# Large products as two weight tiles taking turns, each as three matmuls of 256 columns

## The chip, the cores and the metric

The kernel runs on one core of one Trainium2 chip. The metric is the device time of one execution in microseconds; three runs of the kernel before gave 2638.32, 2636.36 and 2638.91 (median 2638.32). Five engines work side by side, each with its own queue of instructions: TensorE (PE in the profile, with its weight loads apart as PEld), VectorE (DVE), ScalarE (ACT), GpSimd (POOL) and SyncE (SP), which here only issues DMAs. They wait for each other through semaphores.

## The reference

Two residual layers over 256 tokens of width 2048, in float32, each followed by a gated feed-forward block with a causal convolution. Layer 0 has an RG-LRU group beside an RWKV-7 group, layer 1 an mLSTM.

```python
def rglru_rwkv7_layer(x, norm, w_in, ..., w_out):
    h = rms_norm(x, norm)
    xa, ga, pb = jnp.split(h @ w_in, [A_WIDTH, 2 * A_WIDTH], axis=-1)
    ya = rg_lru(causal_dwconv(xa, ...), ...) * jax.nn.gelu(ga)
    yb = rwkv7_time_mix(pb, ...)
    return x + jnp.concatenate([ya, yb], axis=-1) @ w_out

def mlstm_layer(x, norm, w_in, ..., w_out):
    xm, z = jnp.split(rms_norm(x, norm) @ w_in, [C_WIDTH], axis=-1)
    ...
    return x + (hs * jax.nn.silu(z)) @ w_out

def conv_ffn(x, norm, w_gate, w_up, conv_w, conv_b, w_down):
    h = rms_norm(x, norm)
    u = jax.nn.silu(causal_dwconv(h @ w_gate, conv_w, conv_b)) * (h @ w_up)
    return x + u @ w_down
```

The products with `w_in`, `w_out`, `w_gate`, `w_up` and `w_down` are the large ones: 436 MB of weights, each used once.

## The kernel before

Activations lie transposed, features on the 128 partitions and the T = 256 tokens along the free dimension, in tiles of 128 features. A product of `nk` input tiles by `nm` output tiles takes `nk` x `nm` weight tiles of 128x128. To keep float32 accuracy with float32r operands, weights and activations are split into a rounded part and a rest: `w = hi + lo`, and an activation tile is `x[:, 1]` (rounded) and `x[:, 0]` (rest). Each weight tile adds three products of 256 columns to its output: `hi`·`x0`, `hi`·`x1` and `lo`·`x1`.

`chunk` (L192) loads 16 weight tiles (1 MB) with one DMA of SP into a `raw` buffer (two of them) and splits them in four pieces: ACT copies 512 columns to `wh`, DVE subtracts to `wl` (L201, L202). `wh` and `wl` have two buffers each.

There are three ways to run a product:

- **Wide, one accumulator** (`project` and `flat` with `mm3`, L205): one matmul of 512 columns (`hi` with both halves of x) into a whole `[128, 2, 256]` accumulator, and one of 256 (`lo` with `x1`) into its second half. The two halves are added when the result is drained. Used for the mLSTM's input (`oin`, 64 output tiles of 16) and for the output products (`oout`, 16 of 32; `eoa` and `eob`, 16 of 8 each). The accumulators come from a pool of three (`mm`).
- **Narrow, one accumulator** (`EWIDE` False): three matmuls of 256 columns into one `[128, 256]` sum (L216 to L218). Used for layer 0's input (`ein`, 40 output tiles of 16) and for the low-rank products at the start (`elow`).
- **Wide pairs** (`flat_pairs` with `mm3_pair`, L258): two output tiles at once, with two accumulators: both 512s (L263), then both 256s (L265). Used for the feed-forward block: `fgu` (gate and up, 44 pairs of 16) and `fd` (down, 8 pairs of 44), in both layers. Their accumulators are a pool of two pairs (`mp`).

Draining a wide result into an activation (`scaled`, L365) takes an ACT copy of one half, a DVE addition of the other and a DVE multiplication by `rstd`; a narrow one takes the multiplication alone. `add_residual` (L382) takes two DVE additions for a wide result and one for a narrow one.

The recurrences run as generators: after every fourth weight tile `tick` lets each of them emit its next piece, so that their small products stand between the large ones on TensorE. `finish` ticks with no large products in between; `even` calls it for the last RWKV pairs between `eoa` and `eob`. A scheduler then sets each engine's order; it moves instructions past each other where their operands allow.

At the start (`load_x`, L128) the four pieces of x and the four `elow` chunks are loaded in turns by SP. GpSimd squares x and sums the squares for the norm.

Of the kernel before, what the change touches and what calls it, by code (L numbers as in the profile page):

```python
# [24 lines left out]
P = 128  # L25
# [19 lines left out]
EWIDE = False  # L45
# [3 lines left out]
AWAITS = [0, 4, 0, 1, 1, 3]  # L49

# [56 lines left out]
class Builder:  # L107
# [115 lines left out]
    def project(self, src, wide=True):  # L223

        w = self.chunk(src)
        ps = self.psum_mm()
        ps = ps if wide else ps[:, 0]
        for k in range(KD):
            self.mm3(ps, w, slice(k * P, k * P + P), self.x[k], k == 0, k == KD - 1)
            if k % TICK == TICK - 1:  # L230
                self.tick()
        return ps

    def projections(self, src, n, wide=True):

        ahead = [self.project(src[i], wide) for i in range(2)]
        yield from ahead
        for i in range(2, n):
            yield self.project(src[i], wide)

    def flat(self, src, nk, nm, x, done):

        w, ps = None, None
        for i in range(nm * nk):
            m, k = divmod(i, nk)
            if i % 16 == 0:
                w = self.chunk(src[i // 16])
            if k == 0:
                ps = self.psum_mm()
            c = i % 16 * P  # L250
            self.mm3(ps, w, slice(c, c + P), x[k], k == 0, k == nk - 1)
            if k == nk - 1:
                done(m, ps)
            if i % TICK == TICK - 1:
                self.tick()


    def mm3_pair(self, ps, w, c, x, start, stop):  # L258
        TE = self.nc.tensor
        hi = [w[0][:, i:i + P] for i in c]  # L260
        lo = [w[1][:, i:i + P] for i in c]
        for i in range(2):
            TE.matmul(ps[:, i], hi[i], x, start=start, stop=False)  # L263
        for i in range(2):
            TE.matmul(ps[:, i, 1], lo[i], x[:, 1], start=False, stop=stop)  # L265

    def flat_pairs(self, src, nk, npair, x, pool):

        w, ps = None, None
        for i in range(npair * nk):  # L270
            k = i % nk
            if i % 8 == 0:
                w = self.chunk(src[i // 8])
            if k == 0:
                ps = pool.tile([P, 2, 2, T], F32, name=self.name("mp"), tag="mp")
            c = i % 8 * 2 * P
            self.mm3_pair(ps, w, (c, c + P), x[k], k == 0, k == nk - 1)
            if i % 2 == 1:
                self.tick()
            if k == nk - 1:  # L280
                yield ps
# [100 lines left out]
    def add_residual(self, m, ps, gain):  # L382
        for i in range(2):
            self.nc.vector.tensor_tensor(out=self.res[m], in0=ps[:, i], in1=self.res[m], op=ALU.add)  # L384
        if gain is not False:
            self.norm_tile(m, gain)


    def ffn(self, l, gain):
        nc, tc = self.nc, self.tc  # L390
        with ExitStack() as es:
            big = es.enter_context(self.tile_pool(name=f"ffn{l}", bufs=1))
            tmp = es.enter_context(self.tile_pool(name=f"ffnt{l}", bufs=2))
            nps = es.enter_context(self.tile_pool(name=f"ffn_ps{l}", bufs=1, space=PSUM))
            pps = es.enter_context(self.tile_pool(name=f"ffn_pp{l}", bufs=2, space=PSUM))
# [4 lines left out]
            ahead = [next(pairs) for _ in range(2)]  # L400
            for f, ps in enumerate(chain(ahead, pairs)):
                g = self.scaled(tmp, ps[:, 0], 2, "g")
                c = self.conv(tmp, g, 3, f"f_conv_w{l}", NF, f"f_conv_b{l}", f, "cv")
                nc.scalar.activation(c, c, AF.Silu)
                u = self.scaled(tmp, ps[:, 1], 0, "u")
                nc.vector.tensor_tensor(out=u, in0=u, in1=c, op=ALU.mult)
                ux.append(big.tile([P, 2, T], F32R, name=self.name("ux"), tag=f"u{f}"))
                self.split(u, ux[f])
            for m, ps in enumerate(self.flat_pairs(self.io[f"fd{l}"], NF, KD // 2, ux, pps)):
                for i in range(2):  # L410
                    self.add_residual(2 * m + i, ps[:, i], gain)


    def even(self, gain):
        nc, tc = self.nc, self.tc
        with ExitStack() as es:
# [14 lines left out]
            ps = self.projections(ein, 40, EWIDE)  # L431
# [368 lines left out]
    def odd(self, gain, folded, fold_pool):  # L800
# [3 lines left out]
        with ExitStack() as es:  # L804
# [5 lines left out]
            with ExitStack() as e1:  # L810
# [9 lines left out]
                ps = self.projections(io["oin"], CHEADS * CTILES)  # L820
# [14 lines left out]
            with ExitStack() as e2:  # L835
# [7 lines left out]
                nums = self.start(self.heads_out(one, sml, pw, pst, gates, raws, vs, xcs, zs, big_tile, yx))  # L843
                for ct in range(CHEADS * CTILES):
                    while len(zs) >= 6:
                        self.tick()
                    z = self.scaled(sml, self.project(io["oin"][32 + ct]), 0, "z", 6)
                    A.activation(z, z, AF.Silu)
                    zs[ct] = z
# [234 lines left out]
def _by_cols(w):  # L1084

    k, m = w.shape
    return np.ascontiguousarray(w.reshape(k // P, P, m // P, P).transpose(2, 1, 0, 3)).reshape(m // P, P, -1)


def _flat(w):  # L1090

    k, m = w.shape
    t = w.reshape(k // P, P, m // P, P).transpose(2, 0, 1, 3).reshape(-1, 16, P, P)
    return np.ascontiguousarray(t.transpose(0, 2, 1, 3)).reshape(-1, P, 2048)


def _pairs(ws):

    n, k, _, _ = ws.shape
    t = ws.reshape(n, k // P, P, 2, P).transpose(0, 1, 3, 2, 4).reshape(-1, 16, P, P)  # L1100
# [9 lines left out]
def _arrange(I):  # L1110
# [16 lines left out]
    o["ein"] = _by_cols(np.concatenate(pieces, 1))  # L1127
    o["eoa"], o["eob"] = _flat(I["even_w_out"][0][:AW]), _flat(I["even_w_out"][0][AW:])
    o["oin"], o["oout"] = _by_cols(I["odd_w_in"][0]), _flat(I["odd_w_out"][0])
    for l in range(2):  # L1130
        by = lambda n: I[n][l].reshape(D, NF, P).transpose(1, 0, 2)
        o[f"fgu{l}"] = _pairs(np.stack([by("ffn_w_gate"), by("ffn_w_up")], 2))
        o[f"fd{l}"] = _pairs(I["ffn_w_down"][l].reshape(DFF, KD // 2, 2, P).transpose(1, 0, 2, 3))
# [43 lines left out]
```

## Time and profile before

| | us |
|---|---|
| median of three runs | 2638.32 |
| profiled execution | 2638.66 |
| its span, first to last instruction | 2636.9 |
| ein and the recurrences of layer 0 | 35 to 388 |
| eoa, eob | 394 to 517 |
| FFN up and down, layer 0 | 517 to 1251 |
| mLSTM: oin, then oout | 1251 to 1885 |
| FFN up and down, layer 1 | 1885 to 2620 |

The page gives each engine's busy time, the span in 40 slices, the chain of work that ended last, and the costliest groups. A row of a group reads: line, engine, operation, out<-in, shapes, count | busy us, mean ns of one | idle time of the engine before it, and what ended that. In the order of time, a row gives start and length in us, then the same names; `x2` says that two equal instructions follow each other. A matmul's record is longer than the distance to the next one, since matmuls are pipelined: distances are read from starts.

### The profile page before, as it was taken

The page shows a single profiled execution, that of the slowest core. Times are in us where ns is not written, and L with a number is a line of the kernel's source. Part 1 is how long each engine was busy: PE and PEld are TensorE (multiplying, and loading weights), DVE is VectorE, ACT ScalarE, POOL GpSimd, SP SyncE. Part 2 cuts the span into 40 slices and gives each one's busy share as a digit, 9 for nine tenths or more (in the row PEclk, how much of TensorE's full clock was granted, in tenths as well). Part 3 has the DMA queues.
Part 4 walks back from the last instruction along what each step waited for, and adds up shares of the span by engine and source line. Part 5 has one row for each costly group of instructions (what it writes and reads, how often), then busy time and mean ns, then how long its engine had stood idle before and what let it go on. Part 6 is the DMA issues. An engine that isn't in the chain of part 4 may idle for free.

```text
span 2636.9 us, 42747 instructions
## 1 busy us (share of the span) xinstructions
PE 2595.7 (98%) x16200; PEld 2274.7 (86%) x16200; DVE 1872.8 (71%) x4251; ACT 1457.9 (55%) x3078; POOL 163.7 (6%) x442
## 2 busy tenths in 40 slices
PE   7999999999999999999999999999999999999997
PEld 7988887888888888888888888888888888888886
DVE  7988888888666666555777788865666677765554
ACT  5766664555555554444666766644455555554443
POOL 4122121000000000000000000000000000000000
PEclk9999999999999999999999999999999999999998
DMA  5433333465555555555444344455555555555553
GB/s 189 155 123 118 128 103 132 169 213 206 188 191 192 192 192 192 192 192 195 147 149 146 136 160 149 155 183 186 191 192 188 186 187 190 187 188 201 180 201 131
DMA packets 67119, 454.38 MB, mean 172 GB/s; under 512 B 9264, under 2 KB 9776, under 8 KB 13664
## 3 DMA queue, kind: packets, MB, share of 16 engines
q1 hardware_dynamic: 62352, 443.78, 47.2%
q0 software_dynamic: 4416, 7.85, 1.1%
q8 instruction: 127, 2.08, 0.3%
q14 instruction: 80, 0.66, 0.1%
q10 hardware_dynamic: 144, 0.01, 0.0%
HBM read 448.70 MB, written 2.10 MB: 171 GB/s over the span
## 4 chain that ended last, share of the span: by engine, by line
PE 81%; DVE 0%; ACT 0%; POOL 0%; issue 0%; DVEq 0%; POOLq 0%
PE mp L263 37%; PE mp L265 19%; PE mm L214 14%; PE mm L212 7%; PE sc L887 1%; PE mm L211 1%; PE pv L872 1%; PE pz L1027 1%; PE pr L881 1%; PE pz L1028 0%; DVE res L1072 0%; PE pz L1005 0%; PE pt L349 0%; PE pt L1041 0%; PE pt L1018 0%; DVE res L384 0%
## 5 line engine op out<-in xcount | busy, mean ns | idle before, releaser
L202 DVE TENSOR_TENSOR wl<-raw,wh 128x512 fp32r<-128x512 f32 (+1 forms) x1680 | 1102.4, 688 | 506.6 <-ACT wh L201 505.5
L201 ACT CAST wh<-raw 128x512 fp32r<-128x512 f32 (+1 forms) x1680 | 954.0, 617 | 729.7 <-PE mp L263 506.6
L263 PE MATMUL mp<-x,wh 128*128 128x512 f32 x2816 | 884.7, 395 | 0.0
L265 PEld LDWEIGHTS mp<-x,wl 128*128 128x128 f32 x2816 | 529.0, 188 | 125.0
L265 PE MATMUL mp<-x,wl 128*128 128x256 f32 x2816 | 553.2, 278 | 0.0
L263 PE MATMUL mp<-ux,wh 128*128 128x512 f32 x1408 | 436.8, 392 | 0.0
L263 PEld LDWEIGHTS mp<-x,wh 128*128 128x128 f32 x2816 | 428.8, 189 | 0.1
L214 PE MATMUL mm<-x,wh 128*128 128x512 f32 x960 | 341.7, 394 | 0.0
L265 PEld LDWEIGHTS mp<-ux,wl 128*128 128x128 f32 x1408 | 264.4, 188 | 58.1
L212 PE MATMUL mm<-x,wl 128*128 128x256 f32 x1024 | 283.4, 287 | 0.0
L265 PE MATMUL mp<-ux,wl 128*128 128x256 f32 x1408 | 277.8, 279 | 0.0
L214 PE MATMUL mm<-yx,wh 128*128 128x512 f32 x720 | 258.2, 398 | 0.0
L212 PE MATMUL mm<-yx,wl 128*128 128x256 f32 x768 | 211.6, 286 | 1.9 <-DVE wl L202 1.0
L263 PEld LDWEIGHTS mp<-ux,wh 128*128 128x128 f32 x1408 | 213.2, 188 | 0.0
L214 PEld LDWEIGHTS mm<-x,wh 128*128 128x128 f32 x960 | 180.2, 188 | 35.9 <-DVE x L296 0.2
L212 PEld LDWEIGHTS mm<-x,wl 128*128 128x128 f32 x1024 | 193.2, 189 | 7.5 <-DVE yx L175 2.3
L216 PE MATMUL mm<-x,wh 128*128 128x256 f32 x640 | 194.5, 304 | 0.0
L218 PE MATMUL mm<-x,wl 128*128 128x256 f32 x640 | 182.9, 286 | 2.3 <-DVE wl L202 2.3
L217 PE MATMUL mm<-x,wh 128*128 128x256 f32 x640 | 181.6, 284 | 0.0
L214 PEld LDWEIGHTS mm<-yx,wh 128*128 128x128 f32 x720 | 136.4, 190 | 29.2 <-DVE yx L175 0.2
L212 PEld LDWEIGHTS mm<-yx,wl 128*128 128x128 f32 x768 | 145.0, 189 | 7.9 <-DVE wl L202 1.6
L216 PEld LDWEIGHTS mm<-x,wh 128*128 128x128 f32 x640 | 122.4, 191 | 6.9
(352 smaller groups left out, 2656.1 us busy)
## 6 DMA issues: line engine op xcount, KB each, us to landing
raw<-fgu SPq DMA_DIRECT2D x176, 1024.0 KB, 4.8
raw<-fd SPq DMA_DIRECT2D x88, 1024.0 KB, 4.8
raw<-oin SPq DMA_DIRECT2D x64, 1024.0 KB, 4.8
raw<-ein SPq DMA_DIRECT2D x40, 1024.0 KB, 4.9
raw<-oout SPq DMA_DIRECT2D x32, 1024.0 KB, 4.8
raw<-eoa SPq DMA_DIRECT2D x8, 1024.0 KB, 4.8
raw<-eob SPq DMA_DIRECT2D x8, 1024.0 KB, 4.8
wif<-wif POOLq DMA_DIRECT2D x12, 256.0 KB, 4.4
```

The lines of the kernel that those rows point to most:

```text
L201: nc.scalar.copy(hi[:, s], raw[:, s])
L202: nc.vector.tensor_tensor(out=lo[:, s], in0=raw[:, s], in1=hi[:, s].bitcast(F32), op=ALU.subtract)
L211: TE.matmul(ps, hi, x, start=True, stop=False)
L212: TE.matmul(ps[:, 1], lo, x[:, 1], start=False, stop=False)
L214: TE.matmul(ps, hi, x, start=False, stop=stop)
L216: TE.matmul(ps, hi, x[:, 0], start=start, stop=False)
L217: TE.matmul(ps, hi, x[:, 1], start=False, stop=False)
L218: TE.matmul(ps, lo, x[:, 1], start=False, stop=stop)
L263: TE.matmul(ps[:, i], hi[i], x, start=start, stop=False)
L265: TE.matmul(ps[:, i, 1], lo[i], x[:, 1], start=False, stop=stop)
L872: TE.matmul(ps[:, s], xm[:, 3 + s * P:3 + s * P + P], bv, start=True, stop=True)
L881: TE.matmul(ps, bl, xc, start=True, stop=True)
```

## The change

All large products but the start's low-rank ones go through one function, `stream`. It walks through `turns`: the second half of one output tile's weight tiles alternates with the first half of the next output tile's. Within a pair of weight tiles the matmuls alternate too. With `WIDE` False each weight tile is three matmuls of 256 columns into one sum. Weights are laid out in memory in that order (`_stream`), and `oin` becomes two streams, `oxm` and `oz`. The feed-forward block uses the common pool of three accumulators instead of pairs. At the start SP loads the first piece of x and ACT's queue the other three, all ahead of the first weight chunk's use, and the squares are ACT's, with the sums on DVE.

```diff
+def turns(n, nk):
+    h = nk // 2
+    for s in range(n + 1):
+        a = [(s - 1, k) for k in range(h, nk)] if s else []
+        b = [(s, k) for k in range(h)] if s < n else []
+        yield from zip(a, b) if a and b else ((t,) for t in a + b)
...
         for i in range(4):
-            nc.sync.dma_start(out=res[:, 4 * i:4 * i + 4], in_=self.io["xT"][:, 4 * i:4 * i + 4])
+            (nc.scalar if i else nc.sync).dma_start(out=res[:, 4 * i:4 * i + 4], in_=self.io["xT"][:, 4 * i:4 * i + 4])
+        for i in range(4):
             hi, lo = self.chunk(low[i], 4 * w, 4)
             for k in range(4 * i, 4 * i + 4):
                 self.operand(k, gain)
-                self.square(k, nc.gpsimd)
+                self.square(k)
...
+    def stream(self, src, n, nk, x):
+        TE = self.nc.tensor
+        ps, w, at = {}, None, 0
+        for step in turns(n, nk):
+            ops = []
+            for m, k in step:
+                if at % 16 == 0:
+                    w = self.chunk(src[at // 16])
+                c = slice(at % 16 * P, at % 16 * P + P)
+                at += 1
+                if k == 0:
+                    ps[m] = self.psum_mm()
+                ops.append(self.parts_of(ps[m], (w[0][:, c], w[1][:, c]), x[k], k == 0, k == nk - 1))
+            for group in zip(*ops):
+                for out, lhsT, rhs, start, stop in group:
+                    TE.matmul(out, lhsT, rhs, start=start, stop=stop)
+            if at % TICK == 0:
+                self.tick()
+            for m, k in step:
+                if k == nk - 1:
+                    yield ps.pop(m)
+
+    def parts_of(self, ps, w, x, first, last):
+        hi, lo = w
+        if WIDE:
+            return [(ps, hi, x, first, False), (ps[:, 1], lo, x[:, 1], False, last)]
+        ps = ps[:, 0]
+        return [(ps, hi, x[:, 0], first, False), (ps, hi, x[:, 1], False, False), (ps, lo, x[:, 1], False, last)]
...
     def add_residual(self, m, ps, gain):
-        for i in range(2):
-            self.nc.vector.tensor_tensor(out=self.res[m], in0=ps[:, i], in1=self.res[m], op=ALU.add)
+        for p in [ps[:, i] for i in range(2)] if WIDE else [ps]:
+            self.nc.vector.tensor_tensor(out=self.res[m], in0=p, in1=self.res[m], op=ALU.add)
...
-            pairs = self.flat_pairs(self.io[f"fgu{l}"], KD, NF, self.x, pps)
+            ps = self.projections(self.io[f"fgu{l}"], 2 * NF)
...
-            for m, ps in enumerate(self.flat_pairs(self.io[f"fd{l}"], NF, KD // 2, ux, pps)):
-                for i in range(2):
-                    self.add_residual(2 * m + i, ps[:, i], gain)
+            self.flat(self.io[f"fd{l}"], NF, KD, ux, lambda m, ps: self.add_residual(m, ps, gain))
```

How that moves instructions is seen on three engines. On TensorE, in layer 0's FFN up, before (an `mp` is an accumulator pair, `x2` are its two halves, a `wh` and its `wl` hold one chunk):

```order
L263 MATMUL mp_6921<-x_6713,wh_6956 128x512 x2
L265 MATMUL mp_6921<-x_6713,wl_6957 128x256 x2
L263 MATMUL mp_6921<-x_6750,wh_6956 128x512 x2
L265 MATMUL mp_6921<-x_6750,wl_6957 128x256 x2
L263 MATMUL mp_6921<-x_6775,wh_6956 128x512 x2
L265 MATMUL mp_6921<-x_6775,wl_6957 128x256 x2
```

And now, in the same product (an `mm` is one output tile's sum):

```order
L249 MATMUL mm_7130<-x_6449,wh_7089 128x256
L249 MATMUL mm_7062<-x_6752,wh_7089 128x256
L249 MATMUL mm_7130<-x_6449,wh_7089 128x256
L249 MATMUL mm_7062<-x_6752,wl_7090 128x256
L249 MATMUL mm_7130<-x_6449,wl_7090 128x256
L249 MATMUL mm_7062<-x_6796,wh_7089 128x256
L249 MATMUL mm_7130<-x_6492,wh_7089 128x256
```

Four matmuls for two weight tiles have become six, and the two sums that alternate are half an output tile apart in k.

On SP, at the start of the program, before (`xT` is x, `elow` the low-rank weights, `vec` and `con_even` vectors and constants):

```order
L138 DMA res<-xT 128x1024
L195 DMA raw_100<-elow 128x1152
L138 DMA res<-xT 128x1024
L195 DMA raw_172<-elow 128x1152
L138 DMA res<-xT 128x1024
L195 DMA raw_245<-elow 128x1152
L138 DMA res<-xT 128x1024
L195 DMA raw_318<-elow 128x1152
```

And now:

```order
L147 DMA res<-xT 128x1024
L205 DMA raw_103<-elow 128x1152
L205 DMA raw_174<-elow 128x1152
L164 DMA vec_sb<-vec 128x787
L176 DMA con_even_sb<-con_even 128x900
L449 DMA lora_612<-lora 128x256
L205 DMA raw_246<-elow 128x1152
L205 DMA raw_318<-elow 128x1152
```

Three loads of x are gone from SP (they are ACT's second to fourth instructions), and three others stand ahead of the third weight chunk.

On DVE, at the end of eoa, before (L384 adds eoa's results to `res`, `s`, `x` and `uv` belong to a round of the last RWKV pair, L202 splits weights of eob):

```order
L674 TENSOR_TENSOR x_1042_6185<-pc_6186,mv_5544 128x64
L202 TENSOR_TENSOR wl_6289<-raw_6286,wh_6288 128x512
L384 TENSOR_TENSOR res<-mm_6176,res 128x256
L679 COPY uv_5387<-pc_6200 64x64
L384 TENSOR_TENSOR res<-mm_6176,res 128x256
L680 COPY uv_5387<-pc_6200 64x64
L202 TENSOR_TENSOR wl_6350<-raw_6347,wh_6349 128x512
L696 SCALAR_TENSOR_TENSOR s_1046_6208<-pc_6205,pc_5204,sd_6210 64x64 x2
```

And now, around eoa's last result:

```order
L666 TENSOR_TENSOR x_1035_6257<-pc_6258,mv_5577 128x64
L381 TENSOR_TENSOR res<-mm_6187,res 128x256
L671 COPY uv_5467<-pc_6274 64x64
L672 COPY uv_5467<-pc_6274 64x64
L381 TENSOR_TENSOR res<-mm_6244,res 128x256
L688 SCALAR_TENSOR_TENSOR s_1039_6295<-pc_6292,pc_5229,sd_6297 64x64 x2
L212 TENSOR_TENSOR wl_6470<-raw_6467,wh_6469 128x512
L666 TENSOR_TENSOR x_1042_6307<-pc_6308,mv_5577 128x64
```

The round's `x_1042` stood ahead of eoa's last result and now stands behind it.

More of the change, by code (lines that the diff above doesn't have):

```diff
@@ L44 @@
 ZSTEP = 7
-EWIDE = False
+WIDE = False
 PIECES = 4
@@ new lines, in parts_of, with result, projections @@
+    def parts_of(self, ps, w, x, first, last):
[4 more added lines that the diff above has]
+        return [(ps, hi, x[:, 0], first, False), (ps, hi, x[:, 1], False, False), (ps, lo, x[:, 1], False, last)]
+    def result(self, ps):
+        return ps if WIDE else ps[:, 0]
+    def projections(self, src, n):
+        g = self.stream(src, n, KD, self.x)
+        ahead = [self.result(next(g)) for i in range(2)]
@@ L237, in projections @@
         yield from ahead
-        for i in range(2, n):
-            yield self.project(src[i], wide)
+        for ps in g:
+            yield self.result(ps)
     def flat(self, src, nk, nm, x, done):
[L243 to L255, printed above, removed]
@@ L258, in mm3_pair @@
[L258 to L261, printed above, removed]
-        for i in range(2):
-            TE.matmul(ps[:, i], hi[i], x, start=start, stop=False)
-        for i in range(2):
[L265 to L281, printed above, removed]
+        for m, ps in enumerate(self.stream(src, nm, nk, x)):
+            done(m, self.result(ps))
@@ L430, in even @@
             self.load_con("con_even", E, nc.sync)
-            ps = self.projections(ein, 40, EWIDE)
+            ps = self.projections(ein, 40)
             ahead = next(ps)
@@ L846, in odd @@
                         self.tick()
-                    z = self.scaled(sml, self.project(io["oin"][32 + ct]), 0, "z", 6)
+                    z = self.scaled(sml, self.result(next(ps)), 0, "z", 6)
                     A.activation(z, z, AF.Silu)
@@ L1080, in trunk_kernel, with _stream @@
     Builder(tc, io, ctx).build()
-def _by_cols(w):
+def _stream(w):
     k, m = w.shape
[L1087 to L1100, printed above, removed]
+    t = w.reshape(k // P, P, m // P, P).transpose(2, 0, 1, 3)
+    i = np.array([x for step in turns(m // P, k // P) for x in step])
+    t = t[i[:, 0], i[:, 1]].reshape(-1, 16, P, P)
     return np.ascontiguousarray(t.transpose(0, 2, 1, 3)).reshape(-1, P, 2048)
@@ L1126, in _arrange @@
         pieces += [w[:, cols(j)], w[:, AW + j * P:AW + j * P + P]]
-    o["ein"] = _by_cols(np.concatenate(pieces, 1))
-    o["eoa"], o["eob"] = _flat(I["even_w_out"][0][:AW]), _flat(I["even_w_out"][0][AW:])
-    o["oin"], o["oout"] = _by_cols(I["odd_w_in"][0]), _flat(I["odd_w_out"][0])
+    o["ein"] = _stream(np.concatenate(pieces, 1))
+    o["eoa"], o["eob"] = _stream(I["even_w_out"][0][:AW]), _stream(I["even_w_out"][0][AW:])
+    o["oxm"], o["oz"] = _stream(I["odd_w_in"][0][:, :CW]), _stream(I["odd_w_in"][0][:, CW:])
+    o["oout"] = _stream(I["odd_w_out"][0])
     for l in range(2):
-        by = lambda n: I[n][l].reshape(D, NF, P).transpose(1, 0, 2)
-        o[f"fgu{l}"] = _pairs(np.stack([by("ffn_w_gate"), by("ffn_w_up")], 2))
-        o[f"fd{l}"] = _pairs(I["ffn_w_down"][l].reshape(DFF, KD // 2, 2, P).transpose(1, 0, 2, 3))
+        gu = np.stack([I[n][l].reshape(D, NF, P) for n in ("ffn_w_gate", "ffn_w_up")], 2)
+        o[f"fgu{l}"], o[f"fd{l}"] = _stream(gu.reshape(D, 2 * DFF)), _stream(I["ffn_w_down"][l])
     lora = z(8, P, 4, P)
```

25 lines of the change are left out of this document (6 added, 19 removed).

## The prediction

> **What bounds the kernel now.** I read the page from its busy times to its chain, then the busy time by stage, then single matmuls in order of time.
>
> ```profile
> span 2636.9 us, 42747 instructions
> PE 2595.7 (98%) x16200; PEld 2274.7 (86%) x16200; DVE 1872.8 (71%) x4251; ACT 1457.9 (55%) x3078; POOL 163.7 (6%) x442
> PE   7999999999999999999999999999999999999997
> PEld 7988887888888888888888888888888888888886
> PEclk9999999999999999999999999999999999999998
> PE 81%; DVE 0%; ACT 0%; POOL 0%; issue 0%; DVEq 0%; POOLq 0%
> ```
>
> TensorE is busy in every slice but the first and the last, at the full granted clock, and the chain that ended last runs through almost nothing else. So time is matmuls times their spacing; what other engines save is hidden. Each matmul has a weight load of its own (16200 of both). The busy time is no measure of spacing, as records overlap, so I count records in stretches of one kind of work:
>
> ```profile
> core 0: us, PE busy (x) PEld busy (x) DVE busy (x) ACT busy (x) POOL busy (x), PEclk, DMA share, GB/s
> 83.00:95.00 12.00, 12.00 (x103) 12.00 (x102) 10.58 (x32) 7.41 (x14) 1.83 (x5) 1.00 0.45 129
> 520.00:1000.00 480.00, 480.00 (x2761) 418.95 (x2760) 355.69 (x753) 267.71 (x562) 11.40 (x55) 1.00 0.56 198
> 1010.00:1250.00 240.00, 240.00 (x1393) 211.34 (x1392) 131.97 (x237) 106.97 (x206) 0.77 (x3) 1.00 0.54 191
> 1720.00:1880.00 160.00, 160.00 (x914) 139.80 (x913) 92.99 (x172) 71.53 (x142) 0.00 (x0) 1.00 0.55 192
> ```
>
> The rows are: ein (already three matmuls of 256 columns per weight tile), FFN up, FFN down (both pairs of wide tiles), and oout (wide tiles, one accumulator). A record is counted if it touches the stretch, so the count belongs to the stretch plus one record (0.28 us in ein, 0.34 on average elsewhere). That gives 12.28/103 = 0.119 us a matmul in ein, 480.34/2761 = 0.1740 in FFN up, 240.34/1393 = 0.1725 in FFN down, 160.34/914 = 0.1754 in oout. Per 128x128 weight tile, with three matmuls in ein and two elsewhere: **ein 0.358, FFN up 0.348, FFN down 0.345, oout 0.351 us.** In ein, weight loading alone fills the whole stretch; elsewhere it leaves an eighth free.
>
> **The change part by part.** The products hold 6,656 weight tiles: FFN up 2,816, FFN down 1,408, oin 1,024, ein 640, oout 512, eoa and eob 256. All but ein go from a 512-column and a 256-column matmul to three of 256. The columns stay at 768 a tile; what is added is 6,016 matmuls, each with a weight load. So one number decides: the spacing of 256-column matmuls that alternate between two accumulators and follow each other without a wider one between. Nothing in this trace is exactly that. The nearest rows:
>
> ```profile
> 60.20 0.28 PE L217 MATMUL mm<-x,wh 128*128 128x256 f32 x1
> 60.31 0.27 PE L218 MATMUL mm<-x,wl 128*128 128x256 f32 x1
> 60.43 0.28 PE L216 MATMUL mm<-x,wh 128*128 128x256 f32 x1
> ...
> 62.10 0.28 PE L218 MATMUL mm<-x,wl 128*128 128x256 f32 x1
> 62.22 0.28 PE L216 MATMUL mm<-x,wh 128*128 128x256 f32 x1
> 62.34 0.28 PE L217 MATMUL mm<-x,wh 128*128 128x256 f32 x1
> ```
>
> ein, one accumulator: just after a break 0.115, but after some seven matmuls it settles at 0.120 and stays.
>
> ```profile
> 18.40 0.28 PE L216 MATMUL pc<-x,wh 128*128 128x256 f32 x1
> ...
> 20.88 0.28 PE L216 MATMUL pc<-x,wh 128*128 128x256 f32 x1
> ```
>
> The low-rank products at the start, three accumulators by turns of three: 21 matmuls in 2.48 us, 0.118; but a third of their loads bring 32 columns only.
>
> ```profile
> 1000.20 0.40 PE L265 MATMUL mp<-x,wl 128*128 128x256 f32 x2
> 1000.43 0.63 PE L263 MATMUL mp<-x,wh 128*128 128x512 f32 x2
> 1000.90 0.39 PE L265 MATMUL mp<-x,wl 128*128 128x256 f32 x2
> 1001.13 0.62 PE L263 MATMUL mp<-x,wh 128*128 128x512 f32 x2
> ```
>
> FFN up: two of 256 on alternating accumulators take 0.23, 0.116 each; but two of 512 went ahead of them, 0.235 each, twice the time their loads need.
>
> ```profile
> L263 PEld LDWEIGHTS mp<-x,wh 128*128 128x128 f32 x2816 | 428.8, 189 | 0.1
> ...
> 301.92 0.96 PEld L602 LDWEIGHTS pw<-ar,bk 64*128 64x128 f32 x8
> ```
>
> Small 128-column products: eight loads, the last starting (0.96-0.19)/7 = 0.110 after the one before (one load's record lasts 189 ns). The bounds are thus 0.110 and 0.120. **I take 0.120**, 0.360 a tile: of these rows ein alone has nothing but full loads and 256 columns for longer than ten matmuls, and the faster ones come behind a break or wide matmuls, when loads have had time to spare. Two accumulators then change nothing, as the load is what is full.
>
> Terms: FFN up 2,816 x (0.360-0.348) = +34 us; FFN down 1,408 x (0.360-0.345) = +21; oin, oout, eoa, eob 1,792 x (0.360-0.351) = +16 (oin and eo are mixed with small products, so I use oout's figure). Ein 0. Sum +71.
>
> The Trainium skill, in "TensorE: Matmul & The Clock Gate", section "Back-to-back issue gap", spaces matmuls by N/2.4 + 2.5 ns, 216 for 512 columns and 109 for 256; by it a tile would go from 325 to 328 ns, and the sum would be +15 us instead of +71. The 0.235 and 0.120 above are both longer than it says. Its page "Perfetto Trace Analysis", section "Optimizing Tensor Performance", holds that "Larger matmuls are more efficient than smaller matmuls, when possible", which speaks against the change; the FFN rows show no such gain (0.235 against twice 0.116), the ein rows a small one (twice 0.120).
>
> **The start.** Now x arrives in four pieces behind weight chunks, and ein runs freely from 37.90.
>
> ```profile
> 11.65 0.33 SPq L195 DMA_DIRECT2D raw<-elow  x1
> 37.90 0.39 PE L218 MATMUL mm<-x,wl 128*128 128x256 f32 x1 [2.28 <-DVE wl L202]
> L202 DVE TENSOR_TENSOR wl<-raw,wh 128x512 fp32r<-128x512 f32 x1664 | 1089.6, 686 | 506.6 <-ACT wh L201 505.5
> L296 DVE SCALAR_TENSOR_TENSOR x<-res,vec_sb,x 128x256 fp32r<-128x256 f32 x64 | 36.1, 578 | 7.8 <-ACT x L295 7.5
> L311 DVE TENSOR_TENSOR ssq<-ssq,sq 128x256 f32<-128x256 f32 x60 | 25.1, 419 | 1.4 <-ACT sq L309 1.4
> L202 DVE TENSOR_TENSOR wl<-raw,wh 128x288 fp32r<-128x288 f32 x16 | 12.8, 856 | 0.0
> 7.32 0.89 DVE L296 SCALAR_TENSOR_TENSOR x<-res,vec_sb,x 128x256 fp32r<-128x256 f32 x1 [7.32 <-ACT x L295]
> ```
>
> Afterwards the squares leave GpSimd for ACT and their sums go to DVE, which becomes the longest lane: 16 splits, 16 operands, 15 sums. With GpSimd at work a 288-column split took 856 ns, more than the 686 of a 512-column one, so I scale: 686 x 288/512 = 0.386; then 16 x 0.386 + 16 x 0.578 + 15 x 0.419 = 21.7 us. It starts when the first weight chunk is there, about 8.5, a guess from the 7.32 of before with all of x now coming beside it, and ends near 30; ein's first split behind it puts the free run near 32. **-6 us**, between 0 (data late) and -10. Three loads of x move from SP's queue to ACT's, some 0.4 us of issue each, before ACT has any data. On SP the vectors and constants now pass ahead of the third weight chunk, which waits for a raw buffer anyway (11.65).
>
> **The ends.** Every result comes as one 256-column sum, so two operations a tile go from ACT and DVE; with TensorE the bound, that is worth nothing but at the end:
>
> ```profile
> 2619.64 1.67 DVE L384 TENSOR_TENSOR res<-mp,res 128x256 f32<-128x256 f32 x4 [8.12 <-PE mp L265]
> ```
>
> Of these four additions one is left behind the last matmul, as the second to last tile is done half a tile earlier: **-1.2 us**. Between eoa and eob the last pair of RWKV heads begins half a tile later against the products, so one round of its chain moves behind eoa's last result (DVE rows in the change). Such idle time is small now:
>
> ```profile
> PE pc L729 <- DVE y L725: 1.6, 2, 0.8
> ```
>
> ```profile
> 459.23 0.32 PE L673 MATMUL pc<-s,ar 64*64 64x64 f32 x2
> ...
> 465.13 0.32 PE L673 MATMUL pc<-s,ar 64*64 64x64 f32 x2
> ```
>
> Between products one round takes 5.9 us, so the price lies between 0 and 6; as the first products of eob still run beside it, I take a third, **+2 us**. The profiled execution lasted 2638.66, its span 2636.9 and 1.8 around it, and is 0.3 above the median. Sum: 2638.7 + 71 - 6 - 1 + 2 = **2705 us**.
>
> **The rivals.** (1) Alternation helps a little and 0.118 holds throughout, as in the low-rank rows: a tile is 0.354, the terms +17, +13, +5 and -3 for ein, then -5 for start and ends: 2666. (2) The one that ends on the other side: what settles ein at 0.120 is the single accumulator and not the load, and turns hold the 0.116 of the FFN's pairs. A tile is 0.348: FFN up 0, FFN down +4, the 1,792 tiles -5, ein -6, start and ends -5: **2627**. Every nanosecond is 6,656 x 3 = 20 us, so from there it decides at 0.116 + 12/20,000 = 0.1166 us: below that the kernel is faster. For it speaks that the pairs' 256s are quicker than any on one accumulator; against it that they have slack ahead. (3) Only loads bound, 0.110: a tile is 0.330, the terms -51, -21, -38, -18, with -5: 2506. Against it: no 256-column run of this trace holds under 0.115. The gap of 109 ns in the Trainium skill's "TensorE: Matmul & The Clock Gate", section "Back-to-back issue gap", would make it 2490, an estimate by that page; the rows above are all longer. (4) The forecast, with stalls: three accumulators of one tile, two always open, so a finished result must be drained within one step of the turns, before the tile after next may start. In eoa and eob a step is eight weight tiles, 8 x 0.36 = 2.9 us, hardly more than the four splits of a chunk (4 x 0.686 = 2.7) that can stand before it on DVE, and the matmuls behind the waiting one wait with it. One split's wait in each of 32 tiles is 22 us: 2727. In the FFN a step is 16 tiles, 5.8 us, twice the splits, and nothing stalls; the splits of the next chunk need no result.
>
> **How the numbers follow.** Forecast 0.50, (1) 0.13, (2) 0.14, (3) 0.15, (4) 0.08. The range reaches from a little under (2) to the forecast with a start that wins nothing and a whole round between eoa and eob (2705 + 6 + 4), rounded up: 2615 to 2718. It leaves out (3) and part of (4), 0.2 in all. A measurement of this kernel tells some 0.2%, 5 us, from no change. Faster gets (3) and most of (2), 0.26; same 0.04; slower 0.70.
>
> **What would show it.** Right: in the FFN 0.120 between matmuls, 480 us of FFN up holding 480/0.120 = 4,000 of them, with weight loading busy throughout; ein as before, running freely from 32. Wrong: spacing at 0.116 or under in the FFN, or TensorE waiting on results in eoa.

## The result, and the profile after

The changed kernel takes **2695.80 us** (median of four runs, 2689.29 to 2696.48) against 2637.48 (four runs, 2636.36 to 2638.91): ratio **1.0217, 95% interval 1.0204 to 1.0230**, slower. The forecast was 2705, in a range of 2615 to 2718. The profiled execution is the one of 2696.48. Ratios, here and below, leave out a run that lies more than 1.5% above the fastest of its kernel; that is one run, the 2643.54 us of the kernel without turns at 192.

Of the page after, the lines that answer to those shown of before: span, busy times, two rows of the 40 slices, and the engines' shares of the chain that ended last.

```profile
span 2694.7 us, 54134 instructions
PE 2648.5 (98%) x22216; PEld 2593.5 (96%) x22216; DVE 1798.7 (67%) x3946; ACT 1417.7 (53%) x2856; POOL 157.1 (6%) x411
PEld 7888888999999999999999999999999999999997
PEclk9999999999999999999999999999999999999998
PE 78%; DVE 2%; DMA 1%; issue 0%; ACT 0%; POOL 0%; DVEq 0%; POOLq 0%
```

22216 - 16200 are the 6,016 added matmuls. TensorE still bounds, at the full granted clock; weight loading has gone from 86% to 96%, and VectorE and ScalarE do less. The busy time by stretch, for FFN up and FFN down of layer 0 and for oout, columns as before:

```profile
540.00:1020.00 480.00, 479.61 (x3990) 478.83 (x3990) 321.84 (x619) 239.37 (x457) 7.28 (x47) 1.00 0.54 187
1040.00:1260.00 220.00, 220.00 (x1870) 220.00 (x1869) 113.29 (x197) 95.27 (x184) 0.67 (x2) 1.00 0.53 187
1780.00:1910.00 130.00, 130.00 (x1106) 130.00 (x1105) 71.35 (x128) 58.76 (x116) 0.00 (x0) 1.00 0.53 186
```

By the same count (the stretch and one record of 0.28 us), FFN up has 480.28/3990 = 0.1204 a matmul (0.120, and a few single waits), where some 4,000 records were forecast. But FFN down has 220.28/1870 = **0.1178**, and oout 130.28/1106 = 0.1178: the same shape, the same line, the same full loads, and another figure. That is the surprise of this profile.

Where the time went is read from the first matmul of each stage. In the order of time, of before (ein's free start is in the prediction): eoa, FFN up, FFN down, oin, FFN up, FFN down, and the last product of all.

```profile
388.95 0.48 PE L211 MATMUL mm<-yx,wh 128*128 128x512 f32 x1
516.75 0.39 PE L263 MATMUL mp<-x,wh 128*128 128x512 f32 x1
1008.09 0.40 PE L263 MATMUL mp<-ux,wh 128*128 128x512 f32 x1
1251.01 0.39 PE L211 MATMUL mm<-x,wh 128*128 128x512 f32 x1
1885.19 0.39 PE L263 MATMUL mp<-x,wh 128*128 128x512 f32 x1
2376.52 0.40 PE L263 MATMUL mp<-ux,wh 128*128 128x512 f32 x1
2619.22 0.39 PE L265 MATMUL mp<-ux,wl 128*128 128x256 f32 x2
```

And after, with ein ahead:

```profile
32.23 0.28 PE L249 MATMUL mm<-x,wh 128*128 128x256 f32 x1
391.23 0.39 PE L249 MATMUL mm<-yx,wh 128*128 128x256 f32 x1
518.68 0.28 PE L249 MATMUL mm<-x,wh 128*128 128x256 f32 x1
1027.87 0.28 PE L249 MATMUL mm<-ux,wh 128*128 128x256 f32 x1
1276.62 0.29 PE L249 MATMUL mm<-x,wh 128*128 128x256 f32 x1
1922.14 0.28 PE L249 MATMUL mm<-x,wh 128*128 128x256 f32 x1
2429.89 0.28 PE L249 MATMUL mm<-ux,wh 128*128 128x256 f32 x1
2678.52 0.28 PE L249 MATMUL mm<-ux,wl 128*128 128x256 f32 x1
```

Differences of these starts (before's last matmul is the second of its row, some 0.12 later):

| term, us | forecast | measured |
|---|---|---|
| ein runs freely from (37.90 before) | -6 | -5.7 |
| ein, from there to eoa | 0 | +8.0 |
| eoa and eob, with the round of RWKV between them | +2.3 and +2 | -0.35 |
| FFN up, both layers | +34 | +17.9 and +16.4 |
| FFN down, both layers | +21 | +5.8 and +5.8 |
| oin and oout | +9.2 and +4.6 | +11.3 |
| behind the last matmul | -1.2 | -1.4 |
| sum | +66 | +57.8 |

### The profile page after: what moved, and what is told of

Same layout as the page of the kernel before. It is cut to its first block, busy times and chain, and to the rows that moved or that the text cites. A ratio compares the mean times of both kernels' runs of the same rounds, so it can differ in the third digit from the quotient of the medians.

```text
span 2694.7 us, 54134 instructions
## 1 busy us (share of the span) xinstructions
PE 2648.5 (98%) x22216; PEld 2593.5 (96%) x22216; DVE 1798.7 (67%) x3946; ACT 1417.7 (53%) x2856; POOL 157.1 (6%) x411
## 4 chain that ended last, share of the span: by engine, by line
PE 78%; DVE 2%; DMA 1%; issue 0%; ACT 0%; POOL 0%; DVEq 0%; POOLq 0%
PE mm L249 74%; DMA wif<-wif 1%; PE sc L880 1%; PE pv L865 1%; DVE wl L212 1%; PE pz L1020 1%; PE pr L874 1%; PE pz L1021 0%; DVE wif L941 0%; DVE res L1065 0%; DVE fold_a L947 0%; PE pz L998 0%; DVE ssq L308 0%; DVE x L293 0%; DVE res L381 0%
## 5 line engine op out<-in xcount | busy, mean ns | idle before, releaser
L249 PE MATMUL mm<-x,wh 128*128 128x256 f32 x8960 | 1471.1, 286 | 0.4 <-ACT wh L211 0.4
L249 PEld LDWEIGHTS mm<-x,wh 128*128 128x128 f32 x8960 | 1239.6, 192 | 12.5 <-issue 2.9
L249 PE MATMUL mm<-x,wl 128*128 128x256 f32 x4480 | 911.2, 283 | 0.0
L249 PEld LDWEIGHTS mm<-x,wl 128*128 128x128 f32 x4480 | 700.9, 192 | 1.3 <-DVE wl L212 0.4
L249 PE MATMUL mm<-ux,wh 128*128 128x256 f32 x2816 | 449.2, 280 | 0.0
L249 PEld LDWEIGHTS mm<-ux,wh 128*128 128x128 f32 x2816 | 384.0, 188 | 0.0
L249 PE MATMUL mm<-ux,wl 128*128 128x256 f32 x1408 | 286.2, 279 | 0.0
L249 PE MATMUL mm<-yx,wh 128*128 128x256 f32 x1536 | 254.2, 284 | 3.0 <-DVE yx L185 1.9
L249 PEld LDWEIGHTS mm<-ux,wl 128*128 128x128 f32 x1408 | 218.2, 188 | 0.0
L358 DVE SCALAR_TENSOR_TENSOR cv<-g,vec_sb,cv 128x256 f32<-128x256 f32 x176 | 85.3, 485 | 64.9 <-ACT cv L355 61.9
```

The lines of the kernel that those rows point to most:

```text
L249: TE.matmul(out, lhsT, rhs, start=start, stop=stop)
L358: nc.vector.scalar_tensor_tensor(out=o, in0=xp[:, j:j + T], scalar=self.vec(wname, j * stride + i), in1=o, op0=ALU.mult, op1=ALU.add)
```

## The experiments

All were judged against the kernel before, on the same chip. Two questions stood open: is the load what sets 0.120, and why do two products with the same instructions differ? What differs is where their inputs lie. From the built program, first byte in a partition, and the distance from the weights modulo 256:

```
wh   37184, 45376    wl 53568, 61760
x    86336 and on, inputs of eoa       0
ux  124288 and on (FFN down)          64
inputs of eob (but the last tile)     64
inputs of oout                        64
```

**Everything moved by 64 bytes.** Theory A is the forecast's; B, C and D are three ways in which a place could count.

```diff
-        self.vec_sb = self.const.tile([P, NV], F32, name="vec_sb")
+        self.vec_sb = self.const.tile([P, NV + 16], F32, name="vec_sb")
```

> The changed kernel with 64 unused bytes put into the first constant tile, so that every later buffer of a partition starts 64 bytes higher. In the changed kernel the weight buffers and x start 64 bytes past a multiple of 128, and its matmuls on x come every 0.120 us; the inputs of FFN down, oout and eob start on a multiple of 128 and theirs come every 0.1178. Now x and the weights start on multiples of 128, the inputs of FFN down and oout 64 bytes past. Theory A (the load alone is full, as forecast): addresses do nothing, FFN up 0.120 and FFN down 0.1178 as before, ratio to the kernel before 1.022. Theory B (the moving operand's own place counts): the two swap, FFN up 0.1178, FFN down and oout 0.120; 4,480 tiles win 3 x 0.0022 and 2,050 lose as much, -16 us, ratio 1.016. Theory C (the place against that of the weights counts): again one product is equal and one differs, no swap, FFN up 0.120, ratio 1.022. Theory D (every operand off 128 costs, the weights too): FFN up falls under 0.1178 and FFN down stays near it, ratio under 1.012.

2695.79 us, ratio 1.0224 (1.0209 to 1.0239). FFN up and FFN down by stretch:

```profile
600.00:1000.00 400.00, 400.00 (x3336) 400.00 (x3335) 261.13 (x489) 201.98 (x385) 3.50 (x35) 1.00 0.52 185
1060.00:1260.00 200.00, 200.00 (x1700) 200.00 (x1700) 104.07 (x182) 88.29 (x170) 0.67 (x2) 1.00 0.53 189
```

400.28/3336 = 0.120 and 200.28/1700 = 0.1178: no swap. B and D fall; A and C (the distance) stay.

**No turns.**

```diff
-    h = nk // 2
-    for s in range(n + 1):
...
+    for s in range(n):
+        yield from (((s, k),) for k in range(nk))
```

> The changed kernel without turns: each output tile's weight tiles follow each other, one accumulator at a time, still three matmuls of 256 columns. Theory A (load is full, as forecast) and every theory of addresses: the accumulators don't matter, 0.120 on x and 0.1178 in FFN down and oout, ratio 1.020 to 1.023. Rival (turns help): 0.122 or more in every product, some 40 us slower, ratio 1.037. Rival (turns cost something, an accumulator that changes at each matmul): 0.118 on x, ratio 1.010.

2682.12 us, ratio 1.0177 (1.0160 to 1.0194). Its FFN up, and the first matmuls of ein, eoa and FFN up:

```profile
600.00:1000.00 400.00, 400.00 (x3336) 400.00 (x3335) 254.74 (x488) 195.26 (x383) 3.41 (x34) 1.00 0.51 183
```

```profile
32.95 0.28 PE L246 MATMUL mm<-x,wh 128*128 128x256 f32 x1
...
382.76 0.36 PE L246 MATMUL mm<-yx,wh 128*128 128x256 f32 x1
...
505.56 0.28 PE L246 MATMUL mm<-x,wh 128*128 128x256 f32 x1
```

The count in FFN up is that of the kernel above to the record: one accumulator or two, 0.120. But 14 us are gone, next to none of it in the pure products: ein takes 349.8 (359.0 with turns), eoa and eob 122.8 (127.5). With turns TensorE waits more for the recurrences there. The longest waits of TensorE between 30 and 520 us (total, times, longest), with turns:

```profile
PE pw L767 <- PE mm L249: 3.8, 5, 0.8
PE pw L582 <- ACT uv L575: 3.3, 5, 0.7
PE pw L611 <- DVE ztmp L630: 2.2, 1, 2.2
PE mm L249 <- DVE yx L185: 1.9, 2, 1.7
```

and without:

```profile
PE pw L579 <- ACT uv L572: 4.8, 5, 1.0
PE pc L718 <- DVE y L714: 1.7, 2, 1.0
```

All waits in these 490 us add up to 18.8 and 10.2 us, which is 8.6 of the 13.9; the rest was not followed. The first row names TensorE itself and can't be followed further; the next ones are waits for the recurrences' small products and for an input of a product, not for a drain.

**Fewer columns, whole loads.**

```diff
-        ps = ps[:, 0]
-        return [(ps, hi, x[:, 0], first, False), (ps, hi, x[:, 1], False, False), (ps, lo, x[:, 1], False, last)]
+        ps, n = ps[:, 0], self.cols
+        f = T if first else n
+        return [(ps[:, 0:f], hi, x[:, 0, 0:f], first, False), (ps[:, 0:n], hi, x[:, 1, 0:n], False, False),
+                (ps[:, 0:n], lo, x[:, 1, 0:n], False, last)]
...
+            self.cols = (224, 160)[l]
```

> The changed kernel with fewer columns in the feed-forward products: 224 of 256 in layer 0 and 160 in layer 1, all but the first matmul of each output tile (the last tokens are left out there, so the output is not the reference's). Theory A (the weight load is full): 0.120 between matmuls in FFN up of both layers, as with 256 columns. Theory E (each load adds a constant to the time of its columns; a wide tile of 768 columns and two loads takes 0.348, a narrow one of 768 and three 0.360, so a load is 0.012 and 256 columns are 0.108): 0.1065 in FFN up of layer 0 and 0.080 in layer 1 where TensorE is not waiting for weights. Theory F (load and columns share one way in, 512 bytes of weights and 1024 of columns a partition in 0.120): 0.110 and 0.090.

2639.95 us, ratio 1.0014 (1.0004 to 1.0025). FFN down with 224 columns, then FFN up with 160:

```profile
1060.00:1200.00 140.00, 140.00 (x1256) 140.00 (x1255) 75.78 (x131) 64.35 (x124) 0.00 (x0) 1.00 0.55 198
1920.00:2250.00 330.00, 330.00 (x2954) 330.00 (x2953) 229.90 (x432) 175.15 (x340) 3.81 (x32) 1.00 0.56 198
```

0.1117 and 0.1118, in spite of 64 columns' difference and with inputs at 64 and at 0, with weight loading busy throughout. All three theories miss. A matmul with a whole load has a floor, as A said, but at **0.112**, not 0.120. Between 0.112 and 0.120 it is not the load alone. The run's total time is no measure of fewer columns: early in layer 0's FFN up TensorE stood 17.2 us at one wait, for an input of the norm, and its granted clock was 0.56 to 0.88 from 540 to 590 us; the two stretches above had 1.00.

**Wide tiles in turns.**

```diff
-WIDE = False
+WIDE = True
```

> The changed kernel with its own switch for wide tiles: one matmul of 512 columns and one of 256 a weight tile, in turns as before, for all products, ein too. Theory E (a load adds 0.012 each): a third of the loads is gone, a tile is 0.348 to 0.349 on x as in the pairs of the kernel before, 0.345 in FFN down, so ein also wins 640 x 0.011 = 7 us; with the start and the end of the change 2625 to 2635, ratio 0.995 to 0.999. Theory A (only 256-column matmuls feel the load): the same figures. Rival (turns between distant sums cost, pairs do not): 0.351 as oout had with one accumulator, 2645, ratio 1.003.

2637.79 us, ratio 1.0005 (0.9996 to 1.0014). A gain of 0.1 to 0.5% was expected from ein and the start; none can be told. With the third matmul gone the change's loss is gone. Turns over wide tiles still cost something: in its profiled run eoa began 6.5 us earlier than before (382.45 for 388.95) and oout took 2.6 us less, but eoa and eob took 4.8 more (132.6 for 127.8) and layer 0's FFN up 2.5 more.

**x moved against the weights.** The runs that tell A from C. First by 64, with FFN down's inputs of layer 1 by 32 more:

```diff
+        self.act.tile([P, 16], F32, name="gap")
         res = self.act.tile([P, KD, T], F32, name="res")
...
+            if (0, 8)[l]:
+                big.tile([P, (0, 8)[l]], F32, name=f"gap{l}")
```

> The changed kernel with 64 unused bytes between the weight buffers and the residual, so that x and all that is placed behind it move by 64 bytes and the weights stay, and 32 more ahead of the inputs of FFN down in layer 1. Distances from the weight buffers, modulo 128 bytes: x 64 (was 0), input of FFN down 0 in layer 0 (was 64) and 32 in layer 1, input of oout and of the second half of the output product 0 (was 64). Theory C (the distance decides): FFN up and oin 0.1178 (were 0.120), FFN down of layer 0 and oout 0.120 (were 0.1178); FFN down of layer 1 unknown, between the two. Theory A and whatever depends on the product and not on the place: FFN up 0.120, FFN down and oout 0.1178. In time under theory C: 2,816 + 1,024 tiles win 0.0067 each and 704 + 512 + 128 lose as much, -17 us: 2679.

2670.18 us, one run. FFN up, FFN down of layer 0 and of layer 1:

```profile
600.00:1000.00 400.00, 400.00 (x3398) 400.00 (x3398) 265.73 (x497) 204.21 (x392) 3.48 (x35) 1.00 0.53 188
1060.00:1240.00 180.00, 180.00 (x1520) 180.00 (x1519) 90.98 (x159) 77.38 (x149) 0.00 (x0) 1.00 0.53 187
2430.00:2630.00 200.00, 200.00 (x1707) 200.00 (x1706) 98.05 (x167) 87.07 (x166) 0.00 (x0) 1.00 0.52 186
```

FFN up went from 0.120 to 400.28/3398 = 0.1178, with nothing changed but an empty gap: A falls. FFN down went to 0.1186 at 128 in layer 0, not to the 0.120 of 0, and to 0.1173 at 160 in layer 1: 128 bytes are not the period. The next moved x by 32, and FFN down's inputs of layer 1 by 96 more:

```diff
+        self.act.tile([P, 8], F32, name="gap")
         res = self.act.tile([P, KD, T], F32, name="res")
...
+            if (0, 24)[l]:
+                big.tile([P, (0, 24)[l]], F32, name=f"gap{l}")
```

> The changed kernel with 32 unused bytes ahead of the residual instead, and 96 more ahead of the inputs of FFN down in layer 1. Distances modulo 128: x 32, input of FFN down 96 in layer 0 and 64 in layer 1 (192 modulo 256), input of oout 96. Theory C: FFN down of layer 1 keeps 0.1178 if 128 bytes are the period, and 0.120 or another figure if the period is 256; what 32 and 96 give is open, between 0.1178 and 0.120, the same for both if only the distance to the nearest multiple counts. Theory A: 0.120 in FFN up, 0.1178 in FFN down and oout.

2658.67 us, one run. FFN up (32), FFN down of layer 0 (96) and of layer 1 (192):

```profile
600.00:1000.00 400.00, 400.00 (x3431) 400.00 (x3430) 268.43 (x502) 205.14 (x396) 3.57 (x36) 1.00 0.53 189
1060.00:1240.00 180.00, 180.00 (x1502) 180.00 (x1501) 91.66 (x161) 77.18 (x148) 0.00 (x0) 1.00 0.52 184
2430.00:2620.00 190.00, 190.00 (x1679) 190.00 (x1679) 97.04 (x167) 86.39 (x165) 0.00 (x0) 1.00 0.55 195
```

0.1167, 0.1200, and **0.1133**: the last one is next to the floor of 0.112, at 256 columns.

**Smaller loads.**

```diff
+        if first or last:
+            return [(ps, hi, x[:, 0], first, False), (ps, hi, x[:, 1], False, False), (ps, lo, x[:, 1], False, last)]
+        r = slice(0, self.rows)
+        return [(ps[r], hi[:, r], x[:, 0], False, False), (ps[r], hi[:, r], x[:, 1], False, False),
+                (ps[r], lo[:, r], x[:, 1], False, False)]
...
+            self.rows = (96, 64)[l]
```

> The changed kernel with smaller weight loads in the feed-forward products, all 256 columns kept: 96 of 128 columns of each weight tile in layer 0, 64 in layer 1, but for the first and last weight tile of each output tile (the other features' sums are left out, so the output is not the reference's). A run with 224 and 160 columns and whole loads showed 0.112 between matmuls for both. Theory G (load and columns run side by side, 0.112 and 0.107 each alone, and hinder each other only where both are nearly full): 0.107 to 0.109 in FFN up and down of both layers, wherever x lies. Theory E (each load adds its part to the columns): 0.108 + 0.009 = 0.117 with 96, 0.114 with 64. Theory A (a load's time goes with its size and is the limit, columns alone 0.107): 0.107 in both.

2647.05 us, one run. FFN up with 96 columns of weights and with 64:

```profile
600.00:1000.00 400.00, 400.00 (x3435) 400.00 (x3434) 269.16 (x504) 204.68 (x396) 3.61 (x36) 1.00 0.53 190
1930.00:2360.00 430.00, 430.00 (x3755) 430.00 (x3754) 292.33 (x547) 222.38 (x430) 3.90 (x39) 1.00 0.54 192
```

That is 0.1165 and 0.1146; FFN down has 0.1133 (1591 matmuls in 180 us) and 0.1168 (1458 in 170) by the same count. All below 0.118 where whole loads gave 0.120 and 0.1178, but none below 0.113, and in FFN down the half load is the slower one. G, E and A all miss; what sets these figures stays open.

**The distance moved in the kernel before.** Nothing of the change is in it.

```diff
+        for t in ("ms", "rsq2"):
+            self.act.tile([P, 2], F32, name=t, tag=t)
         res = self.act.tile([P, KD, T], F32, name="res")
```

> The kernel before with two small buffers of the norm (2 x 32 bytes) placed ahead of the residual instead of behind x: x moves by 64 bytes, so that it too lies 64 past the weights modulo 128, and all behind it stays. Nothing else changes. Theory C: FFN up goes from 0.348 a tile to the 0.345 of FFN down, oin likewise, ein from 0.360 to 0.353: 2,816 x 0.0035 + 1,024 x 0.0035 + 640 x 0.0067 = 18 us less, 2618, ratio 0.993. Theory A: no change, 2636. Rival (wide tiles feel another distance than narrow ones): FFN up as before, ein 4 us less, 2632, ratio 0.998.

2629.89 us, ratio **0.9971** (0.9960 to 0.9982). FFN up went to 0.1725 as forecast:

```profile
600.00:1000.00 400.00, 400.00 (x2321) 352.17 (x2320) 290.61 (x606) 224.00 (x473) 5.61 (x39) 1.00 0.54 194
```

With a record of 0.34 that is 400.34/2321. ein and oin, mixed with small products, gave nothing of the 8 us expected of them.

**A map of the distance.**

```diff
+    for s in range(0, n, 2):
+        yield from (((s, k), (s + 1, k)) for k in range(nk))
...
+            gaps = {5 * i: 32 for i in range(1, 9)}
+            gaps[0] = (160, 448)[l]
...
+                if f in gaps:
+                    big.tile([P, gaps[f] // 4], F32, name=f"gap{l}_{f}")
```

> A map of the distance. The changed kernel with another order of turns (two output tiles side by side over the same input tiles), and with the 44 input tiles of FFN down in nine groups of five or four, each group 32 bytes further from the weights than the one before: in layer 0, with three matmuls of 256 columns, distances 224 to 480, in layer 1, with the wide tiles of the kernel before (FFN up there too), 0 to 256. Nothing is left out. Theory C with a period of 256: 256 gives the 0.120 of 0, 288 the 0.1167 of 32, 320 the 0.1178, 352 the 0.120, 384 the 0.1187, 416 the 0.1173, 448 the 0.1133; 224 is not known. With a period of 512 (the bytes that a partition holds of one weight tile) these are new figures. Wide tiles: 0.349 at 0 and 0.345 at 64, as in the kernel before; if they follow the narrow ones, the lowest lies at 192, near 0.340, and 96 is as slow as 0. Theory A: one figure for all groups of a layer.

2700.45 us, one run. Two groups of one output pair in layer 0, 24 matmuls each: distance 256, then 448.

```profile
1161.31 0.64 PE L247 MATMUL mm<-ux,wh 128*128 128x256 f32 x4
...
1164.19 0.28 PE L247 MATMUL mm<-ux,wh 128*128 128x256 f32 x1
...
1182.65 0.62 PE L247 MATMUL mm<-ux,wh 128*128 128x256 f32 x4
...
1185.37 0.28 PE L247 MATMUL mm<-ux,wh 128*128 128x256 f32 x1
```

2.88/24 = 0.120 and 2.72/24 = 0.1133, 20 us apart in the same product. All groups (the fourth tile of each, median over eight output pairs), beside the stages of the other kernels, in ns a matmul:

```
distance        0     32     64     96    128    160    192    224
stages      120.0  116.7  117.8  120.0  118.7  117.3  113.3      -
map             -      -      -      -      -      -      -  118.3
map, +256   120.0  117.8  117.8  120.0  118.8  117.2  113.3  118.0
```

The period is 256 bytes: seven distances come back 256 further on. Only 32 differs, and there the run with x at 32 itself shows both figures in FFN up of layer 0: 28.28/240 = 0.1178 from 528 to 556 us, and the 0.1167 above from 600 us on. Wide tiles in layer 1 of the map, read the same way, took 346.5 to 352.5 ns.

**All inputs at 192.** Constants go behind the weight buffers, two small buffers of the norm ahead of them, and no byte is added.

```diff
-        self.const = pool("const", 1)
+        self.small = pool("small", 1)
         self.raw = pool("raw", 2)
         self.parts = pool("parts", 2)
+        self.const = pool("const", 1)
```

(`ms` and `rsq2` come from `small`.) In the changed kernel:

> The changed kernel with its constants placed behind the weight buffers instead of ahead of them, and two small buffers of the norm ahead: x, and the inputs of FFN down and of all output products, now lie 192 past the weights modulo 256. Instructions, operands and order stay. Theory C with a period of 256 (map: 0.1133 at 192, 0.120 at 0, 0.1178 at 64): FFN up, oin, ein and eoa, 4,608 tiles, win 0.020 each, FFN down, oout and eob, 2,048 tiles, 0.0133: -92 - 27 = -119 us if no other engine becomes the bound; 2576, ratio to the kernel before 0.977. If VectorE bounds the mixed parts (ein, eoa, oin), these win half: 2594. Theory A (load full at 0.120): 2696.

2618.97 us (median of eight runs), ratio **0.9930** (0.9902 to 0.9957). The runs fall in two groups, four from 2607.28 to 2609.51 and four from 2628.43 to 2635.93, and the median lies between them. The same instructions are now faster than the kernel before, by less than forecast. FFN up of layer 0 at its start and later, FFN down of layer 0 and FFN up of layer 1, in the profiled run of 2635.93:

```profile
528.00:550.00 22.00, 22.00 (x197) 22.00 (x195) 17.23 (x41) 11.93 (x23) 2.14 (x6) 1.00 0.64 219
600.00:1000.00 400.00, 400.00 (x3399) 400.00 (x3398) 265.66 (x497) 204.42 (x392) 3.49 (x35) 1.00 0.53 188
1060.00:1240.00 180.00, 180.00 (x1531) 180.00 (x1530) 92.43 (x161) 78.41 (x150) 0.00 (x0) 1.00 0.53 188
1930.00:2370.00 440.00, 440.00 (x3884) 440.00 (x3884) 302.39 (x567) 230.45 (x446) 3.97 (x40) 1.00 0.55 194
```

The same product ran at 0.1133 first (22.28/197 = 0.113) and at 0.1178 later, and layer 1 at 0.1133, with the same distance and the same granted clock: at 192 there are two spacings. They belong to unbroken stretches of matmuls. In this trace each stretch of 40 or more keeps one spacing from end to end, and the spacing changes only where a wait or small matmuls have come between, though not each time. Layer 0 goes to and fro until its last break, at 581.9 us; the 5,863 matmuls from there to the end of FFN down are one stretch at 0.1178. At 0.1133 they would take 5,863 x 0.0045 = 26 us less, 2609.5, the time of the quick group; that those runs went so is argued, as only one run has a trace.

The two spacings are not peculiar to 192. In the run of the map oout reads its inputs at 64, and its first three long stretches went at 0.1178, 0.1133 and 0.1133, the others at 0.1178. The second and the fourth (20.28/179 = 0.1133 and 20.28/172 = 0.118):

```profile
1776.00:1796.00 20.00, 20.00 (x179) 20.00 (x178) 10.18 (x18) 8.43 (x17) 0.00 (x0) 1.00 0.60 205
1820.00:1840.00 20.00, 20.00 (x172) 20.00 (x171) 10.38 (x19) 8.31 (x17) 0.00 (x0) 1.00 0.51 166
```

At 0 every stretch of 40 or more in the changed kernel's trace had 0.120. So the map's 0.1178 at 64 and 0.1133 at 192 are one of two figures each. Products of over 1,400 matmuls without a break ran at 0.1178 each time at 64 (thirteen in six traces), and at 0.1133 seven times in eleven at 192 (three traces). Whether that is the distance or what ran before is not told apart: each FFN down at 64 follows FFN up at 0 without a break. Without turns:

> The same placement in the kernel without turns (one accumulator after the other, three matmuls of 256 columns). That kernel took 2682 in the old placement, with the same spacing in the pure products as with turns and 14 us less in ein, eoa and eob. Theory C: the same -119, 2563, ratio 0.972. If turns matter once the spacing is 0.113: more than 14 us from the kernel with turns.

2596.04 us (median of six runs: four from 2591.45 to 2596.32, then 2618.81 and 2643.54), ratio **0.9859** (0.9831 to 0.9888, without the last): the fastest kernel here, ahead of both. FFN up of layer 0 and oout in its profiled run (2594.20):

```profile
600.00:980.00 380.00, 380.00 (x3355) 380.00 (x3355) 255.07 (x489) 195.50 (x385) 3.39 (x34) 1.00 0.54 194
1780.00:1850.00 70.00, 70.00 (x597) 70.00 (x596) 39.06 (x71) 31.87 (x64) 0.00 (x0) 1.00 0.51 183
```

The feed-forward work ran at 0.1133 but for the first 50 us of layer 0, oout at 0.1178. The two long runs are about 25 and 49 us above the quick ones; one and both of the long feed-forward stretches at 0.1178 would add 26 and 54 (5,865 and 6,251 matmuls x 0.0045). This too is argued. In the kernel before:

> The same placement in the kernel before, wide tiles but for ein. In the map a wide tile took 0.3465 at 192, 0.3465 at 0 and 0.344 to 0.3465 at 64, within the disturbance there. Theory: only ein, narrow, wins, 640 x 0.020 = 13 us, FFN up 0.349 to 0.347 another 6, FFN down loses 3: 2620, ratio 0.994. Rival (wide tiles win as narrow ones do): 0.340 a tile, 2590, ratio 0.982.

2638.20 us, ratio 1.0008 (1.0000 to 1.0017). FFN up and FFN down of layer 0:

```profile
600.00:1000.00 400.00, 400.00 (x2310) 350.91 (x2309) 288.61 (x602) 221.97 (x468) 5.62 (x39) 1.00 0.54 193
1060.00:1240.00 180.00, 180.00 (x1040) 157.88 (x1039) 98.55 (x178) 79.39 (x152) 0.67 (x2) 1.00 0.54 190
```

Wide tiles went from 0.348 to 0.3465 in FFN up and from 0.345 to 0.347 in FFN down, and eoa began 3.2 us earlier where ein was to win 13: no gain. So at this placement the changed kernel beats the kernel before (0.9930, 0.9902 to 0.9957, against 1.0008, 1.0000 to 1.0017), and in the given one it loses. Some 7 us of that are its start and end. Its narrow tiles beat the wide ones' 0.3465 where they ran at 0.1133 (0.340 a tile), and lose to them at 0.1178 (0.353).

## Why the prediction was right, point by point

- **TensorE's spacing bounds, and 6,016 more matmuls decide.** Right. With wide tiles in turns the loss is gone.
- **256-column matmuls settle at 0.120.** Right for FFN up (+34 forecast, +34.3 measured) and for oin (+9.2 and +10.1). Wrong for FFN down, 0.1178, so +11.6 instead of +21, and for oout, 0.1178 too, so +1.2 instead of +4.6. FFN down was the largest miss.
- **"Two accumulators then change nothing, as the load is what is full."** The first half holds: the same count of records without turns. The second is the step that failed. A whole load has a floor of 0.112, and an empty gap of 64 bytes ahead of x takes 0.120 to 0.1178 with the same loads. ein's 0.120 was the right row to read only because FFN up reads the same x from the same place; FFN down, eob and oout read theirs 64 bytes off, and no row of before showed a narrow tile there.
- **ein unchanged.** Wrong by +8.0: turns cost 9.2 us there and 4.7 in eoa and eob, by the kernel without them. The term of +2 for one round of RWKV behind eoa was of this kind; it was sized too small and put in one place only. The result covers it, as eoa and eob take 5.0 us less than before once the turns are gone (122.8 and 127.8); no run shows what wins that.
- **Start and end.** Right: free from 32.23, with VectorE's work on x from 8.45 to 29.4 (forecast: 8.5 to near 30), and 1.4 us less at the end.
- **Rivals.** (1), 0.118 throughout, came true in FFN down, eob and oout, but not by alternation, as it holds without turns. (2) falls with the same run. (3), 0.110, is near what placement allows (0.1133), not what the change did. (4) fell: of TensorE's listed waits in eoa and eob one was for a drain, 1.1 us at eoa's first products, and that was ein's last. The misses of FFN down (-9) and ein (+8) cancelled each other, which flatters the sum.

Of the two rules of the Trainium skill: the 109 ns for 256 columns ("TensorE: Matmul & The Clock Gate", section "Back-to-back issue gap", which gives it for an isolated matmul and says that in a stream loads and matmuls together set the spacing) was held in no run, 113.3 being the lowest. That larger matmuls are more efficient ("Perfetto Trace Analysis", section "Optimizing Tensor Performance") held at the given placement, and at 192 only where narrow tiles ran at 0.1178.

## What to carry to other kernels

Where products with the same instructions show different spacings, compare where their operands lie before explaining the spacing by the instructions; a row that serves as a price must share the placement too, not only the shape. Before giving up a variant that loses by two per cent on spacing, move the moving operand against the weights by multiples of 32 bytes: that adds no instruction, and here it took the ratio from 1.0217 to 0.9930. Take several times of such a variant, and count the spacing stretch by stretch: a short wait can leave all that follows it at another spacing. And a new order of the large products is paid where small ones stand between them, so cost it in those stages, not in the pure ones.

## What was not expected of the hardware

- With full loads of 128 columns and 256 moving columns in float32r, the spacing depends on the distance of the moving operand from the weights modulo 256 bytes: 0.120 at 0 and 96, 0.1187 at 128, 0.1173 at 160, and one of two at 32 (0.1167, 0.1178), 64 and 192 (0.1133, 0.1178). Moving both together by 64 changed nothing. Raw and split weights were always moved together, so the exact pair is not told apart; why it is so stays open.
- Where there are two spacings, an unbroken stretch of matmuls keeps the one that it starts with (5,863 of them at 0.1178 in one trace), and in these traces only a break changes it. What chooses is open; the spread of 2607 to 2636 us is likely this.
- With 224 or 160 columns a matmul with its load takes 0.112. With 96 or 64 columns of weights and 256 moving ones it takes 0.113 to 0.117.
- Wide tiles depend on the distance less: 0.348, 0.345 and 0.3465 at 0, 64 and 192 in FFN up, and 0.3465 to 0.3525 in the map.
